# Three query tiles of the last chunk moved beside the first query blocks, and out-projection weights split earlier

## The chip, the cores and the metric

One core of one Trainium2 chip runs the whole kernel. The time is the device time of one execution in microseconds (us); lower is better. Engines are named as in the profile: PE is TensorE, PEld its weight loads, DVE is VectorE, ACT is ScalarE, POOL is GpSimd, and SP is the engine that issues nearly all DMAs.

## What is computed

The reference is one transformer block on 2048 positions of width 1024. Its steps, cut to what matters here:

```
mod = silu(c) @ ada_w + ada_b                  # six rows of 1024: sh1 sc1 g1 sh2 sc2 g2
h = rmsnorm(x) * (1 + sc1) + sh1
z = h @ w_in                                   # q, k/v of three branches, gates, two LRU inputs
o_nsa = gates * (compressed + selected + windowed attention)   # 8 heads of 64, 2 groups, top 8 blocks of 64
o_lru = gated linear recurrence over the sequence * gelu(zy)
x = x + g1 * ([rmsnorm(o_nsa), rmsnorm(o_lru)] @ w_out)
h = rmsnorm(x) * (1 + sc2) + sh2
x = x + g2 * ((silu(causal_conv(h @ w_gate)) * (h @ w_up)) @ w_down)
out = rmsnorm(x)
```

Every product is made in three matmuls of fp32r operands: each operand is split into a high part (a rounded copy, on ACT) and a low part (the difference, on DVE), and `mm3` adds high*high, high*low and low*high.

## The kernel before

The kernel has three stages, each with its own pools of SBUF and PSUM. A later pool lies over the addresses of the earlier one, and a tile of it can be written once the old tiles at its address are done with; `reserve` fixes the order in which the tags are laid out. The order of instructions on each engine is made when the kernel is built, by a list scheduler with a timing model, from the order of the program; on the chip each engine then runs its list strictly in order, and so does SP with its DMAs.

**Stage a (about 0 to 565 us)** goes over four chunks of 512 positions. `chunk(c, hT)` makes 16 tiles of 128 columns of z (`z_tile`, 24 matmuls each): 14 and 15 (inputs of the compression), 0 to 7 (LRU), 8 to 11 (the four q tiles, two heads each), 12 and 13 (k), and then v. `weights` loads and splits the tile weights three ahead, in the order of `sequence`; the last chunk has its own order, `TAIL`, in which eight compression steps ("c") stand between z tiles. In `TAIL` the q tiles 8 and 9 stand early, and 10 and 11 come last of all, behind v. At the end of a chunk the next chunk's rows are normed and transposed (`norm_x`, `norm_k`). The adaLN blocks 16 to 47 are made by `ada_next`, one at a time: load 512 KB into the single buffer `ad`, 16 small matmuls (`aprb`), one or two more for the columns. It is called after each of the eight LRU tiles and, in all chunks but the last, twice in a row at the chunk's end (behind `v_tiles`). In chunks 1 and 2, `wo_next` scales one 128-row block of w_out by the norm gain and by g1 and writes it to `W_d` in DRAM.

**Stage t (about 565 to 1446 us)** goes over 16 query blocks of 128 (`TILES`) and two groups of heads, 32 units. A unit has `score_steps` (scores, masked minimum on DVE, exponential on ACT, for blocks 4 and up a choice of the top blocks, scaling on POOL) and `value_steps` (transposes on PE, split on ACT and DVE, two matmuls per 128 keys). Unit n's value steps are woven with unit n+1's score steps and with the projection (`project_steps`, 48 matmuls) and the FFN norm (`ffn_norm`, blocks 0 to 3) of the block before. The order of blocks is 4, 0, 5, 1, 6, 2, 7, 3, 8 to 15. The out-projection weights are read from `W_d` beside the first two units (`load_wo`) and split there, on ACT and DVE.

**Stage f (1446 us to the end)** is the convolutional FFN in four chunks of 512.

Of the kernel before, what the change touches and what calls it, by code (L numbers as in the profile page):

```python
# [9 lines left out]
F32 = mybir.dt.float32  # L10
F32R = mybir.dt.float32r
AF = mybir.ActivationFunctionType
OP = mybir.AluOpType
AX = mybir.AxisListType

P = 128
S = 2048
D = 1024
KT = D // P
NCH = 4  # L20
TC = S // NCH
# [13 lines left out]
for _n, _w in VEC_WIDTHS:  # L35
# [7 lines left out]

LOOK = 4

TAIL = [("z", 4), ("c", 0), ("z", 5), ("c", 1), ("z", 6), ("c", 2), ("z", 7), ("c", 3), ("z", 8), ("c", 4), ("z", 9),
        ("c", 5), ("z", 12), ("c", 6), ("z", 13), ("c", 7), ("v", 0), ("v", 1), ("z", 10), ("z", 11)]

TILES = [4, 0, 5, 1, 6, 2, 7, 3] + list(range(8, 16))
TC_ARGS = dict(schedule_with_timeline_sim=True)  # L50


# [1 line left out]
def hymba_block(ctx, tc, x, vecs, rows, ada, w_in, w_v, lru_w, cmp_w1, cmp_w2, w_out, w_gu, w_dn,  # L54
# [4 lines left out]
    sync, act, dve, pool, pe = nc.sync, nc.scalar, nc.vector, nc.gpsimd, nc.tensor  # L59

    cst = ctx.enter_context(tc.tile_pool(name="cst", bufs=1))
    dr = ctx.enter_context(tc.tile_pool(name="dr", bufs=1, space=DRAM))


    Q_d = dr.tile([G, DH, 2, R, S], F32, name="Q_d")
# [3 lines left out]
    L_d = dr.tile([P, 2, 4, S], F32, name="L_d")  # L69
    KC_d = dr.tile([G, 2, DH, P], F32, name="KC_d")  # L70
    X_d = dr.tile([S, D], F32, name="X_d")
    W_d = dr.tile([KT, P, D], F32, name="W_d")
    H_d = dr.tile([P, 2, KT, TC], F32, name="H_d")


# [32 lines left out]
    def reserve(pl, *tags):  # L108

        for tag, nbytes, bufs in tags:  # L110
            pl.tile([P, nbytes // 4], F32, name="lay_" + tag, tag=tag, bufs=bufs)
# [15 lines left out]
    def mm3(ps, pairs, n, total):  # L127

        for (wh, wl), (xh, xl) in pairs:
            for a, b in ((wh, xh), (wh, xl), (wl, xh)):  # L130
                pe.matmul(ps, a, b, start=(n == 0), stop=(n == total - 1))  # L131
                n += 1
        return n
# [86 lines left out]
    with tc.tile_pool(name="a", bufs=1, reuse_waits="tile") as pl, tc.tile_pool(name="ap", bufs=1, space=PSUM, reuse_waits="tile") as pp:  # L220
# [95 lines left out]
        def wo_next():  # L316

            if not woq:
                return
            k = woq.pop(0)  # L320
            g1b = pl.tile([P, D], F32, name=f"g1b{k}", tag="x", bufs=4)
            sync.dma_start(g1b, G1_d)
            raw = pl.tile([P, D], F32, name=f"wor{k}", tag="x", bufs=4)
            sync.dma_start(raw, w_out[k])
            gain = V("nog", k) if k < 4 else V("log", k - 4)
            st = pl.tile([P, D], F32, name=f"wos{k}", tag="st", bufs=3)
            dve.scalar_tensor_tensor(st, raw, gain, g1b, op0=OP.mult, op1=OP.mult)
            sync.dma_start(W_d[k], st)

        def chunk(c, hT):  # L330
            t0 = c * TC
            nxt = None
            for n in range(2):
                ps = z_tile(c, 14 + n, hT, f"zc{c}_{n}")
                st = pl.tile([P, TC], F32, name=f"cs{c}_{n}", tag="xp", bufs=2)

                st = st.rearrange("p (l s) -> p l s", l=16)
                act.activation(st, ps.rearrange("p (s l) -> p l s", l=16), AF.Copy)
                for g in range(G):
                    sync.dma_start(C_d[n, g, :, :, t0 // 16:(t0 + TC) // 16].rearrange("l d s -> d l s"),  # L340
                                   st[g * 64:(g + 1) * 64])
# [15 lines left out]
            for m in range(4):  # L357
                ps = z_tile(c, m, hT, f"zx{c}_{m}")
# [14 lines left out]
            for m in range(4):  # L373
                ps = z_tile(c, 4 + m, hT, f"zy{c}_{m}")
# [53 lines left out]
            def q_tile(j):  # L428
                ps = z_tile(c, 8 + j, hT, f"zq{c}_{j}")
                st = pl.tile([P, 2, TC], F32R, name=f"qs{c}_{j}", tag="st", bufs=3)  # L430
                act.activation(st[:, 0], ps, AF.Copy, scale=-0.125)
                dve.scalar_tensor_tensor(st[:, 1], ps, -0.125, st[:, 0].bitcast(F32), op0=OP.mult, op1=OP.subtract)
                for hh in range(2):
                    h = 2 * j + hh
                    (sync if c + 1 < NCH or j < 3 else pool).dma_start(
                        Q_d[h // 4, :, :, h % 4, t0:t0 + TC], st[hh * 64:(hh + 1) * 64].bitcast(F32))

            def k_tile(n):
# [29 lines left out]
            def zs(js):  # L468
                for j in js:
                    q_tile(j - 8) if j < 12 else k_tile(j - 12)  # L470

            if c + 1 < NCH:
                xs = norm_x(pl, x, c + 1, 4, ("t2", 2))
                zs(range(8, 12))
                lru_out()
                nxt = []

                def following(n):
                    nxt.append(norm_k(pl, pp, xs, c + 1, n, A1, B1, 12))

                for n in range(2):
                    zs([12 + n])
                    following(2 * n)
                    following(2 * n + 1)
                v_tiles(lambda k: following(k + 3) if 1 <= k < 5 else None)
                for _ in range(2):
                    ada_next()
            else:
                for n, j in enumerate((8, 9, 12, 13)):
                    zs([j])  # L490
                    compress_step(4 + n)
                lru_out()
                v_tiles()
                zs((10, 11))
            return nxt


# [67 lines left out]
        hT, wts = [], []  # L565
        FIRST = 4
        for k in range(KT):
# [5 lines left out]
            if k == FIRST:  # L573
                prep(FIRST)
                for n in range(FIRST):
                    j = seq[n][2]
# [25 lines left out]
        for m in range(2):  # L602
            raw = pl.tile([P, 4, P], F32, name=f"lw{m}", tag="ge", bufs=2)
# [7 lines left out]
        for c in range(NCH):  # L611
            hT = chunk(c, hT)
# [7 lines left out]
    with tc.tile_pool(name="t", bufs=1, reuse_waits="tile") as pl, tc.tile_pool(name="tp", bufs=1, space=PSUM, reuse_waits="tile") as pp:  # L620
        reserve(pp, ("s", 4096, 2), ("pt", 2048, 3), ("o", 2048, 1))
        reserve(pl, ("MW", 2560, 1), ("ci", 4 * CW, 2), ("Q", 4096, 2), ("K", 3072, 2), ("ks", 2048, 4),
                ("pc", 12288, 2), ("ps", 4096, 10), ("V", 2560, 2), ("vs", 2048, 3), ("pth", 2048, 4),
                ("ptl", 2048, 4))
        MW = pl.tile([P, 640], F32, name="MW", tag="MW", bufs=1)
        sync.dma_start(MW, mask_w)
        wo = {}

        def load_wo(ks):
            for k in ks:  # L630
                t = pl.tile([P, 2, D], F32R, name=f"wo{k}", tag=f"wo{k}", bufs=1)
                raw = pl.tile([P, D], F32, name=f"wr{k}", tag="ps", bufs=10)
                sync.dma_start(raw, W_d[k])
                act.activation(t[:, 0], raw, AF.Copy)
                dve.tensor_tensor(t[:, 1], raw, t[:, 0].bitcast(F32), op=OP.subtract)
                wo[k] = (t[:, 0], t[:, 1])

        def scores(pieces, Qt, h, name):

# [235 lines left out]
        def weave(*parts):  # L875

            parts = [[g, n, 0, k] for k, (g, n) in enumerate(parts) if g is not None]
            while parts:
                p = min(parts, key=lambda p: ((p[2] + 0.5) / p[1], p[3]))
                try:  # L880
                    next(p[0])
                    p[2] += 1
                except StopIteration:
                    parts.remove(p)

        units = [(i, g) for i in TILES for g in range(G)]
        us = [{} for _ in units]
        for _ in score_steps(*units[0], us[0]):
            pass
        for n, (i, g) in enumerate(units):  # L890
            val = value_steps(i, g, us[n])
            nv = (i + 1) + 1 + min(i + 1, 5) + 1
            sc, extra, ne = None, None, 1
            if n + 1 < len(units):
                sc = score_steps(*units[n + 1], us[n + 1])
                if n < 2:
                    next(val)
                    next(sc)
                    load_wo(range(4 - 4 * n, 8 - 4 * n))
            prev = TILES[n // G - 1] if n >= G else None  # L900
            if prev is not None and g == 0:
                extra, ne = project_steps(prev), 4
            elif prev is not None and prev < 4:
                extra, ne = ffn_norm(prev), 2
            weave((val, nv), (sc, 6 + 4 * ((units[min(n + 1, len(units) - 1)][0] + 8) // 8)), (extra, ne))
            us[n] = None
# [3 lines left out]
    with tc.tile_pool(name="f", bufs=1, reuse_waits="tile") as pl, tc.tile_pool(name="fp", bufs=1, space=PSUM, reuse_waits="tile") as pp:  # L910
# [12 lines left out]
        hT = []  # L923
        for k in range(KT):
            t = [pl.tile([P, TC], F32R, name=f"h0{n}_{k}", tag=n, bufs=8) for n in ("hh", "hl")]
# [3 lines left out]
        for c in range(NCH):  # L929
            gT = []  # L930
            for f in range(NF):
# [17 lines left out]
                h = pl.tile([P, TC], F32R, name=f"gh{c}_{f}", tag="gh", bufs=NF)  # L949
                l = pl.tile([P, TC], F32R, name=f"gl{c}_{f}", tag="gl", bufs=NF)  # L950
# [3 lines left out]
            if c + 1 < NCH:  # L954
                hT = norm_T(pl, pp, X_d, c + 1, A2, B2, 6, 8)
# [123 lines left out]
```

## Time and profile before

| | |
|---|---|
| median of 3 runs | 2939.8 us (2936.51 to 2940.53) |
| the profiled execution's own time | 2934.73 us |
| its span | 2933.0 us |
| PE busy | 2832.0 us (97%) |
| DVE, ACT, POOL busy | 1694.0, 1497.8, 1322.3 us |
| DMA moved | 397.89 MB, mean 136 GB/s |

The span is the trace from the first instruction to the last. PE is busy nearly all the time, so time is gained or lost mostly where PE stands idle (in the timeline: "[idle before <-releaser]") or where its granted clock is below full speed (PEclk 1.00 is 2.4 GHz, 0.50 is 1.2 GHz, and a number between is a mean over the stretch of these two). Matmuls overlap, so the distance between two starts is the cost of one, not its duration.

### The profile page before, as it was taken

The numbers are of one execution on the slowest core, as the hardware profiler recorded it, in microseconds if no ns is written. First come the engines' busy times: TensorE is split into PE (matmuls) and PEld (weight loads), VectorE is DVE, ScalarE is ACT, GpSimd is POOL, SyncE is SP. The second block draws the span as 40 slices with busy tenths as digits, with TensorE's granted clock in tenths as the row PEclk, the third lists the DMA queues.
The fourth block names the chain that finished last, engine by engine and source line by source line (L and its number), as shares of the span: only waits on it lengthen the run. The fifth ranks groups of instructions, "written<-read, shape, count | busy, mean of one in ns | idle before, by whom it ended". The sixth has DMA issues, their size and how long they took to land. (4 is left out here: it accounts for less than half of the span.)

```text
span 2933.0 us, 40574 instructions
## 1 busy us (share of the span) xinstructions
PE 2832.0 (97%) x14436; PEld 2328.3 (79%) x14436; DVE 1694.0 (58%) x3149; ACT 1497.8 (51%) x2686; POOL 1322.3 (45%) x1392
## 2 busy tenths in 40 slices
PE   8999999889999899999999999999999999999998
PEld 6777778777778777888788888888887888888886
DVE  4656657776777888888566621666216662166610
ACT  5656566586777777777633333433334333233322
POOL 1111010166666556565344445544455444554444
PEclk9999999999999999999999999999999999999999
DMA  7576655764544434433533333433324333243332
GB/s 285 177 268 203 242 196 151 225 164 129 138 137 121 123 111 111 116 110 96 190 94 96 104 118 98 140 99 96 128 86 151 94 103 121 88 135 100 97 105 78
DMA packets 256617, 397.89 MB, mean 136 GB/s; under 512 B 41376, under 2 KB 168352, under 8 KB 256416
## 3 DMA queue, kind: packets, MB, share of 16 engines
q1 hardware_dynamic: 255808, 394.12, 43.5%
q8 instruction: 115, 1.88, 0.3%
q0 software_dynamic: 320, 1.05, 0.1%
q14 instruction: 86, 0.70, 0.1%
q10 hardware_dynamic: 288, 0.13, 0.0%
HBM read 342.15 MB, written 53.08 MB: 135 GB/s over the span
## 5 line engine op out<-in xcount | busy, mean ns | idle before, releaser
L787 DVE TENSOR_TENSOR tl<-pt,th 128x512 fp32r<-128x512 f32 (+4 forms) x444 | 295.2, 684 | 46.9 <-ACT th L786 45.0
L944 DVE TENSOR_SCALAR ac<-gp,vec 128x512 f32<-128x512 f32 x88 | 188.5, 2143 | 215.6 <-ACT gp L941 208.5
L786 ACT ACTIVATE th<-pt 128x512 fp32r<-128x512 f32 (+4 forms) x444 | 255.1, 594 | 103.2 <-PE pt L785 98.4
L976 DVE TENSOR_TENSOR o<-pt,o 128x128 f32<-128x128 f32 x128 | 28.3, 284 | 433.1 <-PE pt L973 433.1
L757 POOL TENSOR_SCALAR ps<-ps,rs,gates 128x1024 f32<-128x1024 f32 (+7 forms) x192 | 182.0, 958 | 160.3 <-DVE rs L754 116.4
L952 DVE TENSOR_TENSOR gl<-ac,gh 128x512 fp32r<-128x512 f32 x88 | 209.5, 2381 | 69.4 <-ACT gh L951 69.4
L947 ACT ACTIVATE ac<-ac 128x512 f32<-128x512 f32 x88 | 55.7, 633 | 310.7 <-DVE ac L946 310.7
L751 ACT ACTIVATE ps<-ps,mn 128x1024 f32<-128x1024 f32 (+7 forms) x192 | 171.5, 897 | 51.6 <-DVE mn L651 51.3
L785 PE MATMUL pt<-ident,ps 128*128 128x128 f32 x1088 | 167.4, 275 | 7.8 <-DVE tl L787 6.5
L785 PEld LDWEIGHTS pt<-ident,ps 128*128 128x128 f32 x1088 | 133.0, 141 | 44.1 <-DVE tl L787 13.0
L124 POOL TENSOR_TENSOR wd_0l<-wd,wd_0h 128x1408 fp32r<-128x1408 f32 x32 | 103.1, 3223 | 139.8 <-ACT wd_0h L123 139.8
L646 PE MATMUL ss<-ks,Q 128*128 128x512 f32 (+3 forms) x640 | 162.2, 374 | 4.0 <-DVE mn L651 2.1
L124 POOL TENSOR_TENSOR wd_1l<-wd,wd_1h 128x1408 fp32r<-128x1408 f32 x32 | 103.2, 3224 | 130.8 <-ACT wd_1h L123 113.7
L946 DVE SCALAR_TENSOR_TENSOR ac<-gp,vec,ac 128x512 f32<-128x512 f32 x176 | 136.3, 774 | 6.1
L131 PE MATMUL pd<-gl,wd_0h 128*128 128x512 f32 x352 | 139.7, 397 | 0.0
L646 PEld LDWEIGHTS ss<-ks,Q 128*128 128x128 f32 x640 | 114.5, 191 | 30.1 <-issue 4.4
L131 PE MATMUL pd<-gh,wd_0h 128*128 128x512 f32 x352 | 137.9, 392 | 0.0
L131 PE MATMUL pd<-gl,wd_1h 128*128 128x512 f32 x352 | 137.7, 391 | 0.0
L131 PE MATMUL pd<-gh,wd_0l 128*128 128x512 f32 x352 | 137.5, 391 | 0.0
L131 PE MATMUL pd<-gh,wd_1l 128*128 128x512 f32 x352 | 137.3, 390 | 0.0
L131 PE MATMUL pd<-gh,wd_1h 128*128 128x512 f32 x352 | 137.2, 390 | 0.0
L123 ACT ACTIVATE wd_0h<-wd 128x1408 fp32r<-128x1408 f32 x32 | 44.2, 1383 | 158.2 <-PE pd L131 99.8
(1557 smaller groups left out, 8621.8 us busy)
## 6 DMA issues: line engine op xcount, KB each, us to landing
wg<-in_w_gu_dram SPq DMA_DIRECT2D x88, 512.0 KB, 3.6
wu<-in_w_gu_dram SPq DMA_DIRECT2D x88, 512.0 KB, 3.6
wd<-in_w_dn_dram SPq DMA_DIRECT2D x64, 704.0 KB, 4.1
wr<-in_w_in_dram SPq DMA_DIRECT2D x64, 512.0 KB, 5.1
ad<-in_ada_dram SPq DMA_DIRECT2D x32, 512.0 KB, 4.8
Q<-Q_d SPq DMA_DIRECT2D x64, 256.0 KB, 4.5
ks<-K_d SPq DMA_DIRECT2D x56, 256.0 KB, 3.4
vs<-V_d SPq DMA_DIRECT2D x56, 256.0 KB, 3.1
```

Source lines behind the costliest of these rows:

```text
L124: (lo_eng or dve).tensor_tensor(l, raw, h.bitcast(F32), op=OP.subtract)
L131: pe.matmul(ps, a, b, start=(n == 0), stop=(n == total - 1))
L646: pe.matmul(ps[:, o:o + W], Qt[:, hl, h * P:(h + 1) * P], K_ap, start=(hl == 0), stop=(hl == 1))
L751: act.activation(p, p, AF.Exp, scale=-1.0, bias=init, accum_out=sm[:, h, 2 + n:3 + n])
L757: pool.tensor_scalar(p, p, rs[:, h, 2:3], gt[:, h, 1:2], op0=OP.mult, op1=OP.mult)
L785: pe.transpose(pt[:, h * P:(h + 1) * P], jobs[n][0](h), ident)
L786: act.activation(th, pt, AF.Copy)
L787: dve.tensor_tensor(tl, pt, th.bitcast(F32), op=OP.subtract)
L944: dve.tensor_scalar(ac, gp[:, 0:TC], V("fcw", f), V("fcb", f), op0=OP.mult, op1=OP.add)
L946: dve.scalar_tensor_tensor(ac, gp[:, k:k + TC], V("fcw", k * NF + f), ac, op0=OP.mult, op1=OP.add)
L947: act.activation(ac, ac, AF.Silu)
L952: dve.tensor_tensor(l, ac, h.bitcast(F32), op=OP.subtract)
```

## The change

Five things change together.

1. In the last chunk, q tiles 9, 10 and 11 (`LATE`) are no longer made in stage a. The chunk's normed input is written to DRAM (`T_d`, 16 DMAs of 256 KB), and stage t reads it back (4 loads of 1 MB), loads and splits the three tile weights there and makes the three q tiles in 14 steps that are woven with the first four units (`late_steps`). The tiles for this take the SBUF places of `wo0` to `wo6`.
2. `TAIL` is rearranged: v comes before the last compression step, which is now the last PE work of stage a.
3. `wo_next` also splits the scaled block (one more ACT and one more DVE instruction) and writes both parts, 1 MB in place of 512 KB; stage t only loads them, later than before and as their places come free.
4. `ada_next` is called after q tiles 9 and 11 of a chunk, in place of twice behind v.
5. The order of blocks is 2, 0, 3, 1, 4 to 15, and `reserve` of stage t puts `wo0` to `wo4` between `ks` and `pc`.

```diff
-TAIL = [..., ("c", 4), ("z", 9),
-        ("c", 5), ("z", 12), ("c", 6), ("z", 13), ("c", 7), ("v", 0), ("v", 1), ("z", 10), ("z", 11)]
-TILES = [4, 0, 5, 1, 6, 2, 7, 3] + list(range(8, 16))
+TAIL = [..., ("c", 4), ("z", 12),
+        ("c", 5), ("z", 13), ("c", 6), ("v", 0), ("v", 1), ("c", 7)]
+LATE = (1, 2, 3)
+TILES = [2, 0, 3, 1] + list(range(4, 16))
...
-            st = pl.tile([P, D], F32, name=f"wos{k}", tag="st", bufs=3)
-            dve.scalar_tensor_tensor(st, raw, gain, g1b, op0=OP.mult, op1=OP.mult)
-            sync.dma_start(W_d[k], st)
+            dve.scalar_tensor_tensor(raw, raw, gain, g1b, op0=OP.mult, op1=OP.mult)
+            h = pl.tile([P, D], F32R, name=f"wosh{k}", tag="st", bufs=3)
+            l = pl.tile([P, D], F32R, name=f"wosl{k}", tag="st", bufs=3)
+            act.activation(h, raw, AF.Copy)
+            dve.tensor_tensor(l, raw, h.bitcast(F32), op=OP.subtract)
+            sync.dma_start(W_d[k, :, 0, :], h.bitcast(F32))
+            sync.dma_start(W_d[k, :, 1, :], l.bitcast(F32))
...
+            if c + 1 == NCH:
+                for k in range(KT):
+                    for n in range(2):
+                        sync.dma_start(T_d[:, k, n, :], hT[k][n].bitcast(F32))
...
-                zs(range(8, 12))
+                zs((8, 9))
+                ada_next()
+                zs((10, 11))
+                ada_next()
                 lru_out()
...
-                for _ in range(2):
-                    ada_next()
             else:
-                for n, j in enumerate((8, 9, 12, 13)):
+                for n, j in enumerate((8, 12, 13)):
                     zs([j])
                     compress_step(4 + n)
                 lru_out()
                 v_tiles()
-                zs((10, 11))
+                compress_step(7)
...
+                ("wo0", 8192, 1), ("wo1", 8192, 1), ("wo2", 8192, 1), ("wo3", 8192, 1), ("wo4", 8192, 1),
...
-                raw = pl.tile([P, D], F32, name=f"wr{k}", tag="ps", bufs=10)
-                sync.dma_start(raw, W_d[k])
-                act.activation(t[:, 0], raw, AF.Copy)
-                dve.tensor_tensor(t[:, 1], raw, t[:, 0].bitcast(F32), op=OP.subtract)
+                sync.dma_start(t.bitcast(F32), W_d[k])
...
+        def late_steps():
+            hT, W = [], []
+            for k in range(0, KT, 2):
+                t = pl.tile([P, 2, 2, TC], F32R, name=f"hq{k}", tag=f"wo{k // 2}", bufs=1)
+                sync.dma_start(t.bitcast(F32), T_d[:, k:k + 2])
+                hT += [(t[:, n, 0], t[:, n, 1]) for n in range(2)]
+            def weight(n):
+                raw = pl.tile([P, KT, P], F32, name=f"wq{n}", tag="ps", bufs=10)
+                sync.dma_start(raw, w_in[8 + LATE[n]])
+                w = pl.tile([P, 2, KT, P], F32R, name=f"wqs{n}", tag=f"wo{4 + n}", bufs=1)
+                act.activation(w[:, 0], raw, AF.Copy)
+                dve.tensor_tensor(w[:, 1], raw, w[:, 0].bitcast(F32), op=OP.subtract)
+                W.append(w)
+            load_wo([7])
+            for n in range(2):
+                weight(n)
+            for n, j in enumerate(LATE):
+                ps = pp.tile([P, TC], F32, name=f"zl{n}", tag="pt", bufs=3)
+                for k in range(0, KT, 2):
+                    mm3(ps, [((W[n][:, 0, q], W[n][:, 1, q]), hT[q]) for q in (k, k + 1)], 3 * k, 24)
+                    if k + 2 < KT:
+                        yield
+                if n == 0:
+                    weight(2)
+                st = ...  # scaled by -0.125 and split, as in stage a, and written to Q_d on SP
+                load_wo([4 + n])
+                yield
+            load_wo(range(4))
+            yield
...
-        for _ in score_steps(*units[0], us[0]):
-            pass
+        late = late_steps()
+        weave((score_steps(*units[0], us[0]), 6 + 4 * ((units[0][0] + 8) // 8)), (some(late, 3), 3))
...
-                    load_wo(range(4 - 4 * n, 8 - 4 * n))
...
+            if n < 3:
+                extra, ne = some(late, (4, 4, 3)[n]), (4, 4, 3)[n]
+            elif n == 3:
+                extra, ne = chain(project_steps(prev), ffn_norm(prev)), 6
+            elif g == 0:
                 extra, ne = project_steps(prev), 4
```

`some(gen, n)` takes n steps of a generator, and `chain` runs generators one after the other.

## Rows read from the trace of the kernel before

**Rows 1.** The page's first part, busy time, share of the span and instructions of each engine.
```profile
PE 2832.0 (97%) x14436; PEld 2328.3 (79%) x14436; DVE 1694.0 (58%) x3149; ACT 1497.8 (51%) x2686; POOL 1322.3 (45%) x1392
```

**Rows 2.** Windows: stretch; busy us (instructions) of PE, PEld, DVE, ACT, POOL; PEclk; DMA share; GB/s.
```profile
500.00:565.00 65.00, 59.92 (x349) 51.12 (x347) 52.77 (x93) 35.46 (x57) 5.21 (x6) 1.00 0.65 198
...
565.00:705.00 140.00, 118.00 (x624) 93.86 (x625) 99.93 (x349) 98.45 (x260) 81.98 (x140) 0.93 0.61 162
...
705.00:1000.00 295.00, 282.33 (x1562) 230.78 (x1561) 222.82 (x657) 215.48 (x532) 200.65 (x307) 1.00 0.48 132
...
1000.00:1440.00 440.00, 426.96 (x2425) 356.68 (x2423) 361.59 (x959) 327.00 (x702) 242.35 (x335) 1.00 0.40 115
```

**Rows 3.** Waits of PE: total us, times, longest us.
```profile
PE aprb L173 <- DMA ad<-in_ada_dram: 12.8, 6, 3.5
```

**Rows 4.** Timeline of PE at the joints of the chunks: start, us, instruction, idle before.
```profile
141.04 0.65 PE L173 MATMUL aprb<-ad,caz 128*32 128x128 f32 x16 [2.94 <-DMA ad<-in_ada_dram]
...
151.09 1.08 PE L173 MATMUL aprb<-ad,caz 128*32 128x128 f32 x16 [3.53 <-DMA ad<-in_ada_dram]
...
274.35 0.65 PE L173 MATMUL aprb<-ad,caz 128*32 128x128 f32 x16 [3.19 <-DMA ad<-in_ada_dram]
...
402.10 0.64 PE L173 MATMUL aprb<-ad,caz 128*32 128x128 f32 x16 [2.53 <-DMA ad<-in_ada_dram]
```

**Rows 5.** Windows at two of these joints.
```profile
150.00:160.00 10.00, 8.90 (x61) 8.54 (x62) 2.50 (x9) 2.68 (x6) 1.02 (x1) 0.66 0.93 302
...
400.00:410.00 10.00, 7.90 (x62) 7.73 (x63) 4.56 (x8) 9.36 (x16) 4.43 (x9) 0.83 0.99 369
```

**Rows 6.** Timeline of ACT at the three joints, first instruction behind the scaling of x.
```profile
159.87 1.06 ACT L123 ACTIVATE w19h<-wr 128x1024 fp32r<-128x1024 f32 x1 [7.32 <-PE zv L131]
...
287.58 1.06 ACT L123 ACTIVATE w37h<-wr 128x1024 fp32r<-128x1024 f32 x1 [2.32 <-PE zv L131]
...
416.45 1.06 ACT L123 ACTIVATE w55h<-wr 128x1024 fp32r<-128x1024 f32 x1 [2.98 <-PE zv L131]
```

**Rows 7.** Timeline of PE, first matmuls of two z tiles that follow each other.
```profile
446.83 0.40 PE L131 MATMUL zx<-hh,w58h 128*128 128x512 f32 x1
...
452.44 0.39 PE L131 MATMUL zx<-hh,w59h 128*128 128x512 f32 x1
```

**Rows 8.** Tiles wo and zq: count, duration ns min/median/max, first and last start us.
```profile
L634 ACT ACTIVATE wo<-wr x8: 1053/1062/1067, 588.0 to 617.5; 128x1024 fp32r<-128x1024 f32 x8
...
L635 DVE TENSOR_TENSOR wo<-wr,wo x8: 1215/1220/1790, 589.1 to 623.0; 128x1024 fp32r<-128x1024 f32 x8
...
L431 ACT ACTIVATE qs<-zq x16: 575/578/602, 104.9 to 564.8; 128x512 fp32r<-128x512 f32 x16
...
L432 DVE SCALAR_TENSOR_TENSOR qs<-zq,qs x16: 682/684/702, 106.2 to 565.4; 128x512 fp32r<-128x512 f32 x16
```

**Rows 9.** Windows in chunks 1 and 3 and beside the loads of wo.
```profile
200.00:210.00 10.00, 10.00 (x58) 7.77 (x58) 10.00 (x15) 5.67 (x7) 3.76 (x3) 1.00 1.01 383
...
430.00:440.00 10.00, 10.00 (x49) 8.13 (x47) 1.92 (x3) 4.50 (x6) 0.21 (x2) 1.00 0.00 0
...
585.00:590.00 5.00, 4.80 (x28) 3.72 (x28) 4.67 (x15) 3.89 (x10) 1.68 (x2) 1.00 1.00 351
```

**Rows 10.** Timeline of SP at the start of stage t and behind four loads of wo.
```profile
558.86 1.18 SPq L435 DMA_DIRECT2D Q_d<-qs  x2
...
560.13 0.63 SPq L626 DMA_DIRECT2D MW<-in_mask_w_dram  x1
...
613.12 1.80 SPq L673 DMA_DIRECT2D Q<-Q_d  x2
```

**Rows 11.** Timeline of PE: first scores of stage t, a score behind loads of wo.
```profile
568.75 1.61 PE L646 MATMUL sa<-K,Q 128*128 128x340 f32 x8 [3.97 <-DMA K<-K_d]
...
618.87 0.67 PE L646 MATMUL sa<-K,Q 128*128 128x136 f32 x2 [3.60 <-DMA Q<-Q_d]
```

**Rows 12.** Timeline of PE at the start of stage f.
```profile
1448.32 0.50 PE L131 MATMUL pg<-h0hh,wg_0l 128*128 128x512 f32 x1 [1.52 <-DVE wg_0l L124]
```

More of the change, by code (lines that the diff above doesn't have):

```diff
@@ L44 @@
 LOOK = 4
-TAIL = [("z", 4), ("c", 0), ("z", 5), ("c", 1), ("z", 6), ("c", 2), ("z", 7), ("c", 3), ("z", 8), ("c", 4), ("z", 9),
-        ("c", 5), ("z", 12), ("c", 6), ("z", 13), ("c", 7), ("v", 0), ("v", 1), ("z", 10), ("z", 11)]
-TILES = [4, 0, 5, 1, 6, 2, 7, 3] + list(range(8, 16))
+TAIL = [("z", 4), ("c", 0), ("z", 5), ("c", 1), ("z", 6), ("c", 2), ("z", 7), ("c", 3), ("z", 8), ("c", 4), ("z", 12),
+        ("c", 5), ("z", 13), ("c", 6), ("v", 0), ("v", 1), ("c", 7)]
+LATE = (1, 2, 3)
+TILES = [2, 0, 3, 1] + list(range(4, 16))
 TC_ARGS = dict(schedule_with_timeline_sim=True)
@@ L71, in hymba_block @@
     X_d = dr.tile([S, D], F32, name="X_d")
-    W_d = dr.tile([KT, P, D], F32, name="W_d")
+    W_d = dr.tile([KT, P, 2, D], F32, name="W_d")
+    T_d = dr.tile([P, KT, 2, TC], F32, name="T_d")
     H_d = dr.tile([P, 2, KT, TC], F32, name="H_d")
@@ L434, in q_tile @@
                     h = 2 * j + hh
-                    (sync if c + 1 < NCH or j < 3 else pool).dma_start(
+                    sync.dma_start(
                         Q_d[h // 4, :, :, h % 4, t0:t0 + TC], st[hh * 64:(hh + 1) * 64].bitcast(F32))
@@ L631, in load_wo @@
                 t = pl.tile([P, 2, D], F32R, name=f"wo{k}", tag=f"wo{k}", bufs=1)
-                raw = pl.tile([P, D], F32, name=f"wr{k}", tag="ps", bufs=10)
-                sync.dma_start(raw, W_d[k])
-                act.activation(t[:, 0], raw, AF.Copy)
-                dve.tensor_tensor(t[:, 1], raw, t[:, 0].bitcast(F32), op=OP.subtract)
+                sync.dma_start(t.bitcast(F32), W_d[k])
                 wo[k] = (t[:, 0], t[:, 1])
+        def late_steps():
[22 more added lines that the diff above has]
+                    weight(2)
+                st = pl.tile([P, 2, TC], F32R, name=f"ql{n}", tag="ps", bufs=10)
+                act.activation(st[:, 0], ps, AF.Copy, scale=-0.125)
+                dve.scalar_tensor_tensor(st[:, 1], ps, -0.125, st[:, 0].bitcast(F32), op0=OP.mult, op1=OP.subtract)
+                for hh in range(2):
+                    h = 2 * j + hh
+                    sync.dma_start(Q_d[h // 4, :, :, h % 4, S - TC:S], st[hh * 64:(hh + 1) * 64].bitcast(F32))
+                load_wo([4 + n])
+                yield
+            load_wo(range(4))
+            yield
         def scores(pieces, Qt, h, name):
@@ L887, in hymba_block, with some, chain @@
         us = [{} for _ in units]
-        for _ in score_steps(*units[0], us[0]):
-            pass
+        late = late_steps()
+        def some(gen, n):
+            for _ in range(n):
+                next(gen, None)
+                yield
+        def chain(*gens):
+            for gen in gens:
+                yield from gen
+        weave((score_steps(*units[0], us[0]), 6 + 4 * ((units[0][0] + 8) // 8)), (some(late, 3), 3))
         for n, (i, g) in enumerate(units):
@@ L898, in hymba_block @@
                     next(sc)
-                    load_wo(range(4 - 4 * n, 8 - 4 * n))
             prev = TILES[n // G - 1] if n >= G else None
-            if prev is not None and g == 0:
+            if n < 3:
[3 more added lines that the diff above has]
+            elif g == 0:
                 extra, ne = project_steps(prev), 4
-            elif prev is not None and prev < 4:
+            elif prev < 4:
                 extra, ne = ffn_norm(prev), 2
```

## The prediction, made before the changed kernel ran

> **What bounds the kernel now.** I read the page's busy shares first: PE is busy for 97% of the span, so the kernel is bound by PE and at most 101 us of PE's idle time and some slow clock are to be had [rows 1]. The windows then show where. From 1000 to 1440 us PE idles 13.0 of 440 us (3.0%), from 705 to 1000 12.7 of 295 us. From 565 to 705 us, the start of stage t, it idles 22.0 of 140 us at a mean granted clock of 0.93 [rows 2]: 14% of the stretch, 19.6 us, ran at 1.2 GHz, and with PE busy for 84% of it that cost 19.6 * 0.84 / 2 = 8.3 us more. So the start of stage t loses 30.3 us; that is where extra PE work could hide. PE's waits name one other place: six waits of adaLN matmuls for their load, 12.8 us [rows 3], and the timeline puts four of them, 12.2 us, at the joints of the chunks, where `ada_next` is called twice in a row on one buffer [rows 4]. After two of them the clock stood below full [rows 5]: 0.66 over 10 us is 6.8 us at 1.2 GHz, at 89% busy 3.0 us lost; 0.83 is 3.4 us, 1.3 us lost.
>
> **1. adaLN calls spread (part 4).** Removed: at most 12.8 + 3.0 + 1.3 = 17.1 us. What is late next is ACT: at each joint it scales the next chunk's x, which the transposes on PE need, and then stood idle until PE came by, 7.32, 2.32 and 2.98 us [rows 6]. The next chunk can come forward by no more than that, 12.6 us in all. The moved calls stand between q tiles of 5.61 us each [rows 7]; single calls at that spacing hardly wait today (12.8 - 12.2 = 0.6 us of the waits). The matmuls are the same. I take 9 us, nearer the ACT bound than nothing, because ACT's order at the joints changes too. Bounds: 0 and 17.1 us gained.
>
> **2. W_out split in stage a (part 3).** Added in each of chunks 1 and 2: four copies on ACT (4 * 1.06 us) and four subtractions on DVE (4 * 1.22 us) of the shape that stage t has now [rows 8], eight more places taken in the three buffers `st`, and 2 MB more written. They fall into the four zy tiles, 22 us of PE. DVE is full in part of that stretch (10.00 of 10 us) [rows 9], so weight splits there can come late by the added 4.9 us at worst in each chunk. I take +1 us in all; bounds -1 (fewer stalls by luck of order) and +9.8. Removed from stage t: the same 8 * (1.06 + 1.22) us, hidden or not in the loss of 30.3 us, and counted there.
>
> **3. The spill of hT (part 1).** Sixteen DMAs, 4.2 MB written as the chunk's input becomes ready, about 415 to 435 us; at the 351 GB/s seen beside wo's loads that is 12 us of all DMA engines. DMA is idle from 430 to 440 [rows 9] and can take most of it; a weight issued behind it is late if the scheduler puts the spill first. I take +1.5 us; bounds 0 and +8.
>
> **4. The q tiles moved (parts 1, 2).** Three tiles of 5.61 us, 16.8 us of PE [rows 7], leave stage a and come back in stage t.
> The end of stage a does not come forward by all of it. DVE is busy 52.8 of 65 us from 500 to 565 [rows 2], with the LRU's end on it; the three tiles take 3 * (1.22 + 0.68) = 5.7 us from it [rows 8]. The gate of stage t is SP: its first load (MW) went out behind the last q tile's write of the stage on SP, at 560.13 [rows 10], and the first scores began at 568.75 [rows 11]. MW lies over `xc`, which the LRU holds to the end. I take -10 us for the first scores (568.75 to about 558.7): DVE's 5.7 us, and part of the rest because the last compression step no longer has its gelu between the LRU's. Bounds -16.8 and -5.7. That step's own chain (gelu, values) now runs under v and the first loads; on PE it precedes the scores, and `pc` overlies its x buffers, but its matmuls end before the loads land.
> Then 16.8 us of PE work is added. Its cover is the 30.3 us lost today less the 4.0 us of the entry, 26.3 us. Not all is cover: the late tiles need 4.2 MB of hT, `wo7` (1.05 MB, issued ahead) and a weight of 0.5 MB, 5.8 MB behind 1 MB of the block's own loads. At 351 GB/s [rows 9] the 5.8 MB take 16.5 us; from about 550 + 3.5 us on, the first weight lands at 570 and is split (1.06 + 1.22 us [rows 8]) at 572. Until then PE has the scores and first transposes of block 2 alone. Blocks 2, 0, 3, 1 are short, and block 0's two units have less work than their chain takes. I expect 16 of the 26.3 us to stay lost, so 10 to be covered; bounds: 26.3 covered, and 8 more lost.
> Blocks 4 to 7 then run without short ones between. At the 3.0% idle of the later blocks in place of 12.7 us, 295 us would lose 8.9; I take -2, bounds -4 and +4.
> Sum of part 4 with the order of blocks: -10 + 16.8 - 10 - 2 = -5 us. Late copies, q splits and their writes (3 * 2.28 us, 3 * 1.26 us on ACT and DVE, six writes on SP) replace eight wo splits and are the smaller load. SP's later loads queue behind wo's 8.4 MB.
>
> **5. Stage f.** `wo0` and `wo4`, in use to the end of stage t, now lie where stage f puts the last of its h0 parts, its first weight buffer and x. `wo4` is last read at the start of the second half projection and `wo0` 2.2 us before the end, so weight and h0 come just in time beside the 1.52 us wait for the first split [rows 12]; x for the next norm is 5 to 9 us later. I take +1.5 us; bounds 0 and +5.
>
> **Sum.** -9 + 1 + 1.5 - 5 + 1.5 = -10 us. The profiled execution took 2934.73 us (span 2933.0), 5.1 us below the median of the runs; its own time would become 2924.7, and on the median's scale 2939.8 - 10 = 2929.8, so **2930 us**. A difference of 0.2% (5.9 us) is about what can be told from no change.
>
> **The rivals.**
> *All cover is used.* The scheduler places the late matmuls into what are gaps on the chip, and the joints gain all that ACT allows: -12.6 (joints), +1, -10 + 16.8 - 22 - 4 (stage t), +1: about -30 us, 2910. For: 30.3 us lost today [rows 2]. Against: the gaps at the very start are the ones in which the operands have not landed.
> *Moved, not hidden.* The late tiles cost what they cost in stage a and the joints alone gain: -9 + 1 + 1.5 - 10 + 16.8 - 4 + 1.5 = -2 us, 2938. This takes in the case that the adaLN waits only move with their calls. For: the first late matmul comes at 572, where PE today has as much of stage t done.
> *PE waits in order (the other side).* The scheduler's model lands loads early: a Q load issued at 613.12 behind 2 MB of wo held PE until 618.87 for 3.60 us [rows 10, 11]. If it puts the late matmuls ahead of block work that is ready, PE stands before them from about 562 to 572 (+10), and after the last of them waits for `wo6` and `wo0` to `wo3`, 5.2 MB, 14.9 us, with some 8 us of other work (+7), and pays 3 us of half clock. In place of 16 us, 36 stay lost, so part 4 is +15; with -5 at the joints, +1, +1.5 and +1.5 the sum is +14, 2954 us. It decides once the first late matmul lies more than about 5 us ahead of its weight's landing.
> The row shows one load behind another's bytes. The Trainium skill, "DMA: Bandwidth & Descriptors", section "Queues, rings and completion order", has each DMA engine take the descriptors of one ring in order, all of SP's DMAs on one row of rings. By it, the late weight starts only behind the 5.8 MB, which is this rival; if transfers issued together shared the rate evenly, the weight would land some microseconds sooner and the forecast's stall shrink. No row of before settles which.
>
> **How the numbers follow.** Forecast (2924 to 2934) 0.34, all cover 0.20, moved 0.23, waits in order 0.23. Faster by over 0.2% (below 2933.9): 0.34 + 0.20 less the forecast's upper edge, 0.53. Within: 0.24. Slower: 0.23. The range that holds 8 in 10 goes into both outer cases, 2908 to 2952; the forecast's own is 2922 to 2936.
>
> **What would show it.** Step 1: no PE waits on `ad` at the joints, full clock at 150 to 160 us, the first tile of chunk 3 some 9 us earlier. Step 2: DVE's splits in the zy stretches of chunks 1 and 2 without new PE waits. Step 3: no new PE waits for weights in 415 to 440 us. Step 4: first scores about 20 us before today's 568.75 (9 from the joints, 10 from the end of stage a); first late matmul about 14 us behind them; PE's idle and slow clock in the next 140 us some 10 us less. Step 5: an entry to stage f of 1.5 to 3 us of waits. I am wrong if the late matmuls run without a wait right behind the first scores, if PE stands for wo before the first projection, or if the joints gain nothing.

## The result, and the profile after

The changed kernel takes 2964.68 us (median of 6 runs, 2961.1 to 2972.5), the kernel before, beside it, 2938.28: a ratio of 1.0091, 95% interval 1.0078 to 1.0105. It is slower by some 26 us where a time 10 us shorter was forecast, and it lies outside the stated range, beyond its upper end of 2952. The profiled execution took 2962.11 us with a span of 2960.3 (before: 2933.0), so the profile shows 27.3 us to account for.

The page's busy times after, and the first of PE's waits from 100 to 470 us (total us, times, longest us):
```profile
PE 2839.2 (96%) x14436; PEld 2334.9 (79%) x14436; DVE 1688.5 (57%) x3149; ACT 1498.3 (51%) x2686; POOL 1310.2 (44%) x1390
```
```profile
PE aprb L176 <- DMA ad<-in_ada_dram: 8.3, 4, 2.9
```
PE does the same 14436 instructions [rows 1]; its adaLN waits are 8.3 us where they were 12.8 [rows 3]. Windows of the same kernel, columns as in [rows 2]:
```profile
395.00:425.00 30.00, 25.62 (x221) 21.83 (x219) 19.66 (x36) 21.68 (x38) 9.18 (x12) 0.93 0.91 288
565.00:705.00 140.00, 118.01 (x592) 91.75 (x593) 75.46 (x291) 87.37 (x263) 77.74 (x132) 0.89 0.83 242
1440.00:1480.00 40.00, 25.20 (x114) 19.74 (x113) 11.55 (x18) 13.89 (x23) 6.74 (x14) 0.79 0.60 223
```
The kernel before has, over the first of these stretches and over the entry of its stage f:
```profile
395.00:425.00 30.00, 27.07 (x220) 23.84 (x219) 16.70 (x33) 22.55 (x40) 4.84 (x9) 0.94 0.88 293
1430.00:1470.00 40.00, 37.02 (x172) 29.84 (x171) 15.39 (x21) 22.04 (x31) 16.07 (x22) 1.00 0.74 266
```
At the joint of chunks 2 and 3 (395 to 425 us) PE idles 4.4 us where it idled 2.9, at about the same clock: nothing was gained there. From 565 to 705 us PE is as idle as before [rows 2], at a clock of 0.89 in place of 0.93 and with half as much again moved by DMA: the late tiles filled nothing there. The entry of stage f is new as a loss, at a clock of 0.79 where it was 1.00.

Four marks cut the 27.3 us into stages: the first zy tile of chunk 3, the first scores, the end of the last projection, the first gate matmul of stage f. PE's timeline before (the first scores are in [rows 11]), then after:
```profile
459.34 0.39 PE L131 MATMUL zy<-hh,w60h 128*128 128x512 f32 x1
...
1443.35 3.00 PE L131 MATMUL p<-wo,mx 128*128 128x512 f32 x12
1446.18 0.39 PE L131 MATMUL pg<-h0hh,wg_0h 128*128 128x512 f32 x1
```
```profile
465.98 0.39 PE L134 MATMUL zy<-hh,w60h 128*128 128x512 f32 x1
...
568.82 1.73 PE L694 MATMUL sa<-K,Q 128*128 128x408 f32 x4 [4.63 <-DMA K<-K_d]
...
1456.60 2.99 PE L134 MATMUL p<-wo,mx 128*128 128x512 f32 x12
1473.75 0.80 PE L134 MATMUL pg<-h0hh,wg_0h 128*128 128x512 f32 x1 [14.16 <-ACT wg_0h L126]
```

| part | before | after | difference | forecast |
|---|---|---|---|---|
| start to chunk 3's first zy (steps 1 to 3) | 459.3 | 466.0 | +6.6 | -6.5 |
| to the first scores (end of stage a) | 109.4 | 102.8 | -6.6 | -10 |
| stage t to the end of the last projection | 877.6 | 890.8 | +13.2 | +4.8 |
| entry of stage f | -0.2 | 14.2 | +14.3 | +1.5 |
| the rest | 1486.8 | 1486.6 | -0.3 | 0 |

(-6.5 is -9 + 1 + 1.5; +4.8 is 16.8 - 10 - 2.) The first four rows came out above the forecast.

### The profile page after: what moved, and what is told of

Its sections match the earlier page's. It is cut to its first block, busy times and chain, and to the rows that moved or that the text cites. A ratio compares the mean times of both kernels' runs of the same rounds, so it can differ in the third digit from the quotient of the medians.

```text
span 2960.3 us, 40640 instructions
## 1 busy us (share of the span) xinstructions
PE 2839.2 (96%) x14436; PEld 2334.9 (79%) x14436; DVE 1688.5 (57%) x3149; ACT 1498.3 (51%) x2686; POOL 1310.2 (44%) x1390
## 5 line engine op out<-in xcount | busy, mean ns | idle before, releaser
L835 DVE TENSOR_TENSOR tl<-pt,th 128x512 fp32r<-128x512 f32 (+5 forms) x444 | 295.0, 683 | 45.6 <-ACT th L834 42.8
L834 ACT ACTIVATE th<-pt 128x512 fp32r<-128x512 f32 (+5 forms) x444 | 253.5, 591 | 105.1 <-PE pt L833 98.1
L799 ACT ACTIVATE ps<-ps,mn 128x1024 f32<-128x1024 f32 (+7 forms) x192 | 171.1, 895 | 40.1 <-DVE mn L699 39.2
L845 PE MATMUL po<-tl,vs 128*128 128x512 f32 x272 | 123.2, 453 | 2.6 <-DVE tl L835 2.6
```

What stands on the lines that cost most here:

```text
L799: act.activation(p, p, AF.Exp, scale=-1.0, bias=init, accum_out=sm[:, h, 2 + n:3 + n])
L834: act.activation(th, pt, AF.Copy)
L835: dve.tensor_tensor(tl, pt, th.bitcast(F32), op=OP.subtract)
L845: pe.matmul(po, jobs[n][1], tl, start=False, stop=(n == N - 1))
```

## The experiments

Sixteen kernels, each timed beside runs of the kernel before; the ratio to before, given with its 95% interval, is what is compared (it is not exactly the quotient of the medians). All of them are within 1% of before, so what decides is whether the intervals lie apart. The lengths of stages are each read from one profiled execution. Below, the spill is the writing of hT to DRAM (part 1 of the change), the split is part 3, the spread part 4, and the order and the places (of `wo0` to `wo4`, and of stage f) are those of part 5 and e1.

**e1. Other places in stage f.** SP's queue at the end of stage t of the changed kernel, its longest wait there, and what followed:
```profile
1438.26 0.50 SPq L989 DMA_DIRECT2D h0hh<-H_d  x1
...
1439.27 0.43 SPq L989 DMA_DIRECT2D h0hh<-H_d  x1
1457.57 0.32 SPq L989 DMA_DIRECT2D h0hl<-H_d  x1
...
1466.06 0.33 SPq L982 DMA_DIRECT2D wg<-in_w_gu_dram  x1
```
```profile
SPq L989 <- PE p L134: 17.8, 1, 17.8
```
```profile
1472.64 1.06 ACT L126 ACTIVATE wg_0h<-wg 128x1024 fp32r<-128x1024 f32 x1 [17.02 <-DMA wg<-in_w_gu_dram]
```
The fourth of 16 h0 loads waits 17.8 us for the last projection, and twelve loads and the first weight stand behind it.
```diff
-        reserve(pl, ("hh", 2048, 8), ("hl", 2048, 8), ("x", 4096, 6), ("hf", 2048, 2), ("junk", 2048, 1),
-                ("raw", 512 * (NF // 2), 2), ("wh", 512 * (NF // 2), 2), ("wl", 512 * (NF // 2), 2),
+        reserve(pl, ("hh", 2048, 8), ("wh", 512 * (NF // 2), 2), ("gh", 2048, NF), ("hl", 2048, 8),
+                ("raw", 512 * (NF // 2), 2), ("x", 4096, 6), ("wl", 512 * (NF // 2), 2), ("hf", 2048, 2), ("junk", 2048, 1),
```


> The changed kernel, with other places in stage f alone: gh lies over wo0 to wo4, and h0, the first weights and x lie where pc and ps were. Theory A (the fourth of 16 h0 loads waits on SP for the last reader of wo0, 17.8 us, and 12 h0 loads and the first weight wait behind it in order): PE's wait at the entry of stage f falls from 14.2 us to 1.5 to 4 us, the clock there stays full, and the time falls by 11 to 15 us against the changed kernel, to some 2951. Rival B (the loads are late because the DMA engines or H_d's last writes are late, whatever the place): the wait stays over 10 us and the time within 3 us.

2951.51 us, 1.0048 (1.0035 to 1.0062): 13 us of the 26 are gone. PE, DVE, ACT and POOL have the same instructions in the same order as in the changed kernel. PE at the entry, in e1:
```profile
1460.79 2.99 PE L134 MATMUL p<-wo,mx 128*128 128x512 f32 x12
1463.62 0.39 PE L134 MATMUL pg<-h0hh,wg_0h 128*128 128x512 f32 x1
...
1465.76 0.50 PE L134 MATMUL pg<-h0hh,wg_0l 128*128 128x512 f32 x1 [1.51 <-DVE wg_0l L127]
```
The gate matmul follows the projection at once, and what stays is a 1.51 us wait as before [rows 12]. Theory A holds, and rival B is out.

**e2, e3, e4. The joints.** e2 is the changed kernel with the calls put back, e3 the kernel before with the spread alone, e4 with the W_out split alone (diffs as in the change).

> The changed kernel, with the two adaLN calls of each joint back behind the v tiles. Theory A (chunk 3's first zy tile came 6.6 us later than before because of where the adaLN calls lie): it comes 5 to 8 us earlier and the time falls by 5 to 8 us, to some 2957. Rival B (the W_out split and the spill of hT set these 6.6 us): chunk 3's zy tile and the time move by under 2 us.

> The kernel before, with the adaLN calls spread and nothing else. The prediction's step 1: 9 us faster, at most 17.1. Theory A (the scheduler brings the moved calls to the joints again, each behind its own load): no gain, 0 to 7 us slower than before. Rival B (the spread gains and only the W_out split takes it back): 4 to 9 us faster.

> The kernel before, with W_out split in stage a and loaded as two parts, and nothing else. The prediction's step 2: +1 us in stage a (to +9.8), less what stage t gains from 8 copies and 8 subtractions that leave it: -2 to +2 us in all. Rival B (the split costs the 6.6 us that chunk 3 is late): chunk 3's zy tile 4 to 8 us later and the time 3 to 8 us longer.

e2: 2962.86 us, 1.0084 (1.0071 to 1.0097), 2 us less than with the spread, the first zy tile of chunk 3 1.5 us earlier: neither theory's size, nearer to rival B (and the two intervals overlap). e3: 2943.08, 1.0019 (1.0010 to 1.0027): the spread alone costs 5 us, as theory A has it, and PE waits for adaLN loads no less than before (12.8 us in 6 waits [rows 3]):
```profile
PE aprb L173 <- DMA ad<-in_ada_dram: 14.0, 7, 3.2
```
e4: 2935.35, 0.9995 (0.9987 to 1.0004): no cost in all; chunk 3's zy tile is 3.5 us late (the head of chunk 2, from its first zc to its first zy tile, grew from 41.9 to 45.8 us), and stage t is 3.3 us shorter (874.3).

These lengths recur in other runs. The head of chunk 2 takes 44 to 46 us in every kernel with the split and the calls at the joints or spread, and 41 to 42 in those without the split. The head of chunk 3 takes 44.1 to 45.7 us in the five kernels with both the split and the spread (the changed kernel, e1, e5, e7, e8) and 40 to 43 in all others: 41.7 in e2, 40.1 in e3. So where both edits meet, the spread costs some 3 us more there, and the 6.6 us by which chunk 3 came late are the two together, not the spill, which e5 leaves out.

SP's adaLN loads at the joint of chunks 1 and 2, in the kernel before and then in the changed one:
```profile
267.86 0.61 SPq L190 DMA_DIRECT2D ad<-in_ada_dram  x1
275.04 0.33 SPq L190 DMA_DIRECT2D ad<-in_ada_dram  x1
282.08 0.59 SPq L190 DMA_DIRECT2D ad<-in_ada_dram  x1
289.94 0.35 SPq L190 DMA_DIRECT2D ad<-in_ada_dram  x1
295.81 0.34 SPq L190 DMA_DIRECT2D ad<-in_ada_dram  x1
```
```profile
264.59 0.83 SPq L193 DMA_DIRECT2D ad<-in_ada_dram  x1
273.07 1.14 SPq L193 DMA_DIRECT2D ad<-in_ada_dram  x1
282.55 0.33 SPq L193 DMA_DIRECT2D ad<-in_ada_dram  x1
287.52 0.35 SPq L193 DMA_DIRECT2D ad<-in_ada_dram  x1
294.87 0.34 SPq L193 DMA_DIRECT2D ad<-in_ada_dram  x1
```
Five stand at the joint either way, within 3.5 us of where they stood. The blocks are one chain through one buffer, and moving two calls did not shorten it. That the chain lags behind its calls is my reading of these times; no run takes it by itself.

**e5, e6. No late tiles; the order alone.** e5 is the kernel before with the adaLN spread, the W_out split and the blocks' order; e6 has `TILES = [2, 0, 3, 1] + list(range(4, 16))` alone.

> The changed kernel without the late tiles: all q tiles, the order of the last chunk's steps and the places of stage t as before, no spill of hT; the W_out split, the adaLN spread and the blocks' order 2, 0, 3, 1 stay. Theory A (the late tiles' 16.8 us in stage t are covered by about 4 us alone, and stage a's end gives some 6 us back; the entry of stage f is as before): 2938 + 5.4 (adaLN alone) - 2.4 (split alone) + 0 to 4 (order) = 2941 to 2945, some 21 us under the changed kernel and 6 to 10 under that with the other places in stage f. Rival B (the blocks' order costs what the late tiles are blamed for): over 2950.

> The kernel before, with the blocks in the order 2, 0, 3, 1, 4, 5 ... and nothing else. The prediction's term: -2 us (-4 to +4). Theory A: the short blocks then stand at the start with no long block between them, PE idles more from 565 to 705 us and less from 705 to 1000 us; the sum is -2 to +6 us. Rival B: the order is what makes stage t 13 us longer: +10 us or more.

e5: 2940.14 us, 1.0008 (1.0000 to 1.0017), rival B is out; stage t takes 872.0 us, so the late tiles with their loads and places make it 18.8 us longer, more than their own 16.8. e6: 2933.36, 0.9981 (0.9972 to 0.9990): the one edit that gains by itself, 5.6 us by its ratio, more than the forecast's -2 (bound -4) and than theory A. Its one profile does not show where: its span is 2934.0 us, stage t takes 877.8 us as before. And on top of the split the order adds nothing (e9 below, 0.9997, against e4's 0.9995), so its worth lies between nothing and 6 us.

**e7, e8. The late weight first; one unit later.** The wait at the first late matmul, in the changed kernel on SP, ACT and PE:
```profile
565.39 2.02 SPq L653 DMA_DIRECT2D hq<-T_d  x4
568.33 0.32 SPq L645 DMA_DIRECT2D wo<-W_d  x1
568.75 1.22 SPq L658 DMA_DIRECT2D wq<-in_w_in_dram  x2
```
```profile
584.80 1.06 ACT L660 ACTIVATE wqs<-wq 128x1024 fp32r<-128x1024 f32 x1 [7.70 <-DMA wq<-in_w_in_dram]
```
```profile
585.91 1.22 PE L134 MATMUL zl<-hq,wqs 128*128 128x512 f32 x2 [10.38 <-ACT wqs L660]
586.93 1.91 PE L833 MATMUL pt<-ident,pc 128*24 128x128 f32 x8
```
The weight lands 16 us after its issue, and block 2's transposes, whose inputs POOL had ready at about 578, stand behind it in PE's order.
```diff
-            load_wo([7])
-            for n in range(2):
-                weight(n)
+            weight(0)
+            for k in range(0, KT, 2):
+                t = pl.tile([P, 2, 2, TC], F32R, name=f"hq{k}", tag=f"wo{k // 2}", bufs=1)
+                sync.dma_start(t.bitcast(F32), T_d[:, k:k + 2])
+                hT += [(t[:, n, 0], t[:, n, 1]) for n in range(2)]
+            weight(1)
...
-                load_wo([4 + n])
+                load_wo([7, 4] if n == 0 else [4 + n])
```
On top of e1; the loads of hT move here from the start of `late_steps`. e8 adds a `yield` behind `weight(1)` and moves the late steps one unit on.

> The changed kernel with the other places in stage f, and the first late weight issued ahead of hT's four loads, wo7 only behind the first late tile. Theory A (PE stands from 577 to 586 us in order before a late matmul whose weight came behind 5.8 MB): the weight is split by about 573 us, the first late matmul comes by 575 us, PE's wait for it of 10.4 us falls below 3 us, and the time falls by 5 to 9 us, to some 2944. Rival B (hT's loads themselves take as long: the later pairs of matmuls wait in its place, or the block's own loads come late behind them): the time moves by under 3 us.

> As the last, and the late matmuls stand one unit later in the program (none beside the first scores; their loads go out at the same place). Theory A: PE has block 2's transposes and values while hT lands, no wait over 2 us for a late operand, and the time is 7 to 12 us under the changed kernel with the other places, some 2942. Rival B (the cover is lost elsewhere: the late tiles then hold the projections and Q's loads): within 3 us of that kernel.

e7: 2946.87 us, 1.0029 (1.0020 to 1.0038), about 5 us under e1; stage t 885.6. SP, ACT and PE in e7:
```profile
568.20 0.37 SPq L654 DMA_DIRECT2D wq<-in_w_in_dram  x1
```
```profile
574.15 1.06 ACT L656 ACTIVATE wqs<-wq 128x1024 fp32r<-128x1024 f32 x1
```
```profile
575.16 1.70 PE L693 MATMUL ss<-ks,Q 128*128 128x384 f32 x4
576.73 2.18 PE L134 MATMUL zl<-hq,wqs 128*128 128x512 f32 x6
```
The 10.38 us wait is gone and half of it is gained, the lower end of theory A. e8: 2956.20, 1.0063 (1.0050 to 1.0075), 9 us worse than e7: both theories missed.

**e9 to e12.** e9 is the split and the order; e10 the kernel before without the two calls of each joint (`for _ in range(2): ada_next()` goes, the last chunk's calls take the blocks left over); e11 both; e12 is e7 with one late tile (`LATE = (3,)`), the adaLN calls as before; its other two q tiles stand at the very end of stage a, behind the last compression step.

> The kernel before, with the W_out split in stage a and the blocks' order 2, 0, 3, 1; adaLN calls, q tiles and places as before. Theory A (both work on PE's idle time and slow clock of stage t's first 160 us, 877.6 us of stage t before, 874.3 and 877.8 with one of them, 872.0 with both and the adaLN spread): stage t takes 872 to 874 us, stage a stays some 3 us longer; the time is 3 to 6 us under before, 2932 to 2935. Rival B (the gains add up fully): 5 us or more.

> The kernel before, with the two adaLN calls of each joint gone; what is left of the 32 blocks comes with the calls of the last chunk. Theory A (the loads of the adaLN blocks form one chain through the one buffer, an interval of 10 to 14 us in the tiles and 5 to 8 us at the joint, in the kernel before and with the spread alike, to within 2 us; what helps the joint is fewer blocks in a chunk, not another place): three adaLN loads lie between a chunk's last q tile and the next chunk's first zy tile in place of five, PE's waits for them fall from 12.8 us to 4 to 8, and the time falls by 4 to 10 us, if chunk 3 hides its own. Rival B (DVE and ACT at the joint set its length, the adaLN waits only lie in their shadow): under 3 us.

> The kernel before with the W_out split, the blocks' order and no adaLN calls at the joints. Theory A: the gains of the last two add up, 6 to 14 us under before. Rival B (the split's copies take the room that the adaLN calls leave at the joints): like the split and the order alone, 2932 to 2935.

> The changed kernel with one late q tile (j = 3) in place of three, its weight issued first, the other places in stage f, and the adaLN calls as before. Theory A (the idle time of stage t's start lies where the late operands have not landed, so that each late tile costs stage t its 5.6 us and more and gives stage a some 2 us): 2937 to 2943, no better than without late tiles (the split and the order alone). Rival B (there is cover for one tile, and it is the 6.3 MB for three that spoil it): 3 us or more under the split and the order alone.

e9: 2936.26 us, 0.9997 (0.9989 to 1.0006), stage t 874.0, first scores at 573.9 us: stage t as theory A has it, but the time misses its 2932 to 2935, since stage a is 5 us longer. e10: 2939.73, 1.0009 (0.9998 to 1.0020). Its chunk 3 starts its zy tiles 10.0 us earlier (449.34), with this left of the adaLN waits up to 470 us:
```profile
PE aprb L173 <- DMA ad<-in_ada_dram: 3.1, 1, 3.1
```
So the joints did hold 9 us, as step 1 has it. But the blocks left over make the end of chunk 3 6.4 us longer. Stage t, with PE's instructions in the same order, took 5.1 us more in this profile; in e11 and e16, with the same edit, it did not (871.3 and 874.3). e11: 2936.09, 0.9996 (0.9987 to 1.0005), like the split and the order alone, rival B. e12: 2955.16, 1.0062 (1.0048 to 1.0075): a kernel with one late tile is slower than e7 with three, beyond theory A's 2937 to 2943. It differs from e7 in the end of stage a and the adaLN calls as well; but its stage t, counted from the first scores, takes 890.8 us against 885.6. The first 140 us from the first scores in e7, e8 and e12:
```profile
571.43:711.43 140.00, 128.99 (x634) 101.01 (x635) 82.39 (x315) 94.47 (x288) 86.05 (x147) 0.92 0.83 245
572.27:712.27 140.00, 122.73 (x568) 93.85 (x568) 72.54 (x274) 81.82 (x242) 73.08 (x126) 0.84 0.77 226
575.40:715.40 140.00, 124.85 (x568) 93.21 (x569) 77.87 (x301) 89.53 (x276) 83.27 (x144) 0.86 0.75 225
```
PE idles 11.0, 17.3 and 15.2 us and is granted 0.92, 0.84 and 0.86 of its clock. So most of what e8 and e12 lose lies at the start of stage t, as idle time and as slow clock; what makes it is not shown. Fewer late matmuls did not lower the price, and the next runs took the loads by themselves.

**e13 to e16.** On e9: e13 has the spill, hT's loads and the other places, but multiplies nothing late; e14 the places alone; e15 the spill alone. e16 is e6 with e10's edit.
```diff
         for _ in score_steps(*units[0], us[0]):
             pass
+        for k in range(0, KT, 2):
+            t = pl.tile([P, 2, 2, TC], F32R, name=f"hq{k}", tag=f"wo{k // 2}", bufs=1)
+            sync.dma_start(t.bitcast(F32), T_d[:, k:k + 2])
```


> The split and the order, with hT's spill, its four loads into the places of wo0 to wo3 behind the first block's loads, and the other places of stages t and f; all q tiles in stage a, no late matmul. Theory A (the price of the late tiles is the transfer: 4.2 MB more ahead of the loads that block 2 and 0 need): stage t takes 884 to 890 us against 874.0, the time is 2946 to 2952. Rival B (PE's order and the matmuls are the price): within 3 us of the split and the order alone, 2936.

> The split and the order, with wo0 to wo4 between ks and pc in stage t and the other places in stage f; no spill, no loads of hT, no late matmul. Theory A (places cost nothing by themselves): 2934 to 2940. Rival B (wo0 to wo4 and pc then wait for other tenants of stage a, and the first scores or transposes come late): 2944 or more.

> The split and the order, with the 16 writes of hT at the start of chunk 3 and nothing that reads them. The prediction's step 3: +1.5 us (0 to +8). By the head of chunk 3 in the runs so far (45.5 with it, 44.1 without): +1 to +2 us, 2937 to 2939; rival: over 4 us.

> The kernel before with the blocks' order 2, 0, 3, 1 and no adaLN calls at the joints. Theory A (the two edits gain in different stages, -2.6 us and -3.6 us at the first scores): 2930 to 2934. Rival B (what stage a gains, the start of stage t loses, as when the calls at the joints were dropped alone): 2934 to 2940.

e13: 2946.11 us, 1.0028 (1.0017 to 1.0040); e14: 2938.61, 1.0004 (0.9995 to 1.0013); e15: 2940.70, 1.0007 (0.9998 to 1.0017). Stage t: 882.5 with the loads, 875.0 with the places alone, 875.9 with the spill alone. With hT loaded back stage t is 7 to 8 us longer though nothing reads it, a little less than theory A's 884; e14 and e15 are as their theories had them, to 2 us. The start of stage t in e9 and e14, then in e13:
```profile
560.00:720.00 160.00, 143.05 (x717) 109.53 (x716) 95.94 (x363) 105.86 (x314) 104.25 (x176) 0.93 0.74 209
560.00:720.00 160.00, 141.94 (x703) 109.48 (x703) 92.17 (x355) 105.20 (x310) 103.47 (x175) 0.90 0.73 204
```
```profile
560.00:720.00 160.00, 142.77 (x655) 106.04 (x655) 87.69 (x338) 98.96 (x296) 94.82 (x163) 0.88 0.78 226
```
PE is busy as long and shows 62 instructions less than in e9, 48 less than in e14: much of the loss shows as clock. From the two levels, 0.88 is 24% of the stretch at 1.2 GHz and 0.93 is 14%, 16 us more, which at 89% busy costs some 7 us; against e14's 0.90 it is 6.4 us more and some 3 us.

Two things keep this from being the price of the transfer alone. e9, e14 and e15 run PE, DVE, ACT and POOL in one and the same order (stage t 874.0 to 875.9 us), but in e13 the scheduler has put stage t in another order, so loads and order changed together; and e6, which loads no hT, shows a clock of 0.88 in the same stretch too. By the timed runs e13 is 9 us above e9; places and spill by themselves are 2 and 3 of these, within their intervals, which leaves some 4 for loads and order.

e16: 2931.91 us, 0.9990 (0.9981 to 0.9998), in theory A's range; by its ratio it does not beat the order alone.

## Why the prediction was wrong

**Step 5 failed by 13 us**, as the prediction put it: "`wo0` and `wo4` [...] lie where stage f puts the last of its h0 parts". The fourth part lay over `wo0`, not the last. I laid the parts out in the order of their names: by it the fourth would lie over `ks`, which the scores read, but its wait ended with the last projection, so the places of a tag are given out in another order. I also priced each overlap by what reads that place, and not by SP's queue, where a load that waits holds all behind it. +1.5 us was 14.3; e1 takes 13 of it back by places alone.

**Step 1 failed in sign**, by some 14 us: -9 was forecast, and the spread alone cost 5 us (e3). The waits and their worth were right: fewer blocks in a chunk bring chunk 3 forward by 10.0 us (e10). That the spread would remove them was wrong, since "single calls at that spacing hardly wait today" took a call's place in the program for the time at which its block runs. The loads hardly moved, and the waits were 14.0 us in e3 where they had been 12.8. Why the spread costs, and does not just leave things as they are, stays open; that chunk 3's head is some 3 us longer where it meets the split is a place, not a cause.

**Steps 2 and 3** stayed inside their bounds: chunk 3 late by 3.5 us with the split alone (forecast +1, bound +9.8), returned by stage t, and the spill with a ratio 0.0010 above e9's, 3 us, in intervals that overlap (forecast +1.5).

**Step 4, stage a's end:** -6.6 us of -10 (-7.2 to -7.8 in e1, e7 and e8). It came out near the bound that the prediction took from DVE, 5.7 us: in the changed kernel PE ended the v tiles, then stood for the LRU's last sum.
```profile
553.40 0.29 PE L134 MATMUL zv<-w75h,hl 128*128 128x280 f32 x1
560.51 1.87 PE L433 MATMUL pr<-ones,sqs 128*128 128x1 f32 x8 [6.82 <-DVE sqs L418]
```
**Step 4, stage t:** the cover of 10 us was not there. Part of it went to step 2, which shortens stage t by itself (3.3 us in e4's profile). The loads of hT, with the order that the scheduler makes for them, take 4 to 8 us, a term that the sum did not have: I priced them by when they land, and not by what they change in the rest of the stage. And the late matmuls waited 10.38 us in PE's order; e7 gains half of it back. The rival "PE waits in order" had that place and size ("PE stands before them from about 562 to 572 (+10)"; it stood from 575.5 to 585.9); its +15 for part 4 came out as +6.6, with the end of stage a in it, since PE never waited for `wo` and stage t grew by 13.2 us where the rival's sum has 24.8 (the forecast's 4.8 and 20 us more lost). Its total of 2954 us came nearest of all four, but it has -5 us at the joints and +1.5 at stage f, and both of these terms were wrong. The weight landed 16 us after its issue, behind the 5.2 MB of hT and `wo7`, and by 574.15 us, 6 us after its issue, when it went first (e7). The rule of the Trainium skill that stood beside this rival, the page "DMA: Bandwidth & Descriptors", section "Queues, rings and completion order", that a DMA engine takes the descriptors of one ring in order, agrees with this.

With the weight first stage t takes 885.6 us against 882.5 with the loads alone (e13), 3 us for 16.8 us of matmuls. By this pair of profiles most of the matmuls hide, and what comes with them eats the gain: the two kernels' times are the same, 1.0029 and 1.0028. e12 speaks against reading more into it: one tile with the same loads takes 890.8. Why e12 and e8 start stage t with more idle time and less clock than e7 stays open.

Neither kernel is the best here: the order of the blocks, alone (0.9981 of before) or without the joints' calls (e16, 0.9990), is the one part whose interval lies below 1.

## What to carry to other kernels

Before a tile is put where a later stage has its own, take the later stage's loads in the queue's order and ask what the first that must wait holds up (here one h0 part held twelve others and a weight). Work that is moved under a stage brings its operands along, so price the transport by running it alone, without the work, and see whether the scheduler kept the order of the rest. And a call's place in the program is not when it runs: read from the trace where the loads of such a chain stand now, and whether an edit shortens the chain.

## What was not expected of the hardware

A stage with the same matmuls took 7 to 8 us longer with loads beside it that nothing reads, in the order that came with them (e13 against e14 and e15), at a granted clock of 0.88 in place of 0.90 to 0.93. And one program's executions differ by more than some edits do: e1, e7 and e8 have the changed kernel's order on PE up to the first scores, and their chunk 3 came to its zy tiles at 470.3, 469.8 and 470.5 us where the changed kernel's profile has 466.0. A difference of 4 us between two single profiles is therefore not to be read as an edit's price without the timed runs, or the same length in further profiles, beside it.
